# Reordering small VectorE, ScalarE and GpSimd work in a TensorE-bound decoder layer

## The chip, the cores and the metric

The kernel runs on one core of one Trainium2 chip. The metric is the device time of one execution in microseconds, as the median of three runs. A profile of one more execution gives the rows shown below.

## The reference

One decoder layer over x (512 tokens, 1024 features) and a memory of 256 rows, all in float32. Norms are RMS norms with a gain vector.

```
u = rms_norm(x, ln_mix_pre);  proj = u @ w_in            # q, k, v of three branches, three gates
y_swa = windowed attention (8 query heads, 2 key heads, sinks, relative bias)
y_sb  = stick-breaking attention (8 heads of 64):
        a = exp(log_sigmoid(z) + reverse cumulative sum of log_sigmoid(-z)), below the diagonal
y_mem = cross attention to rms_norm(mem, ln_mem) @ w_mem_kv (4 heads of 128)
merged = sum over the branches of sigmoid(gate_b) * (y_b @ w_branch_b)
h = x + rms_norm(merged @ w_out, ln_mix_post)
u = rms_norm(h, ln_ffn_pre)
a = silu(u @ w_gate) * (u @ w_up)
out = h + rms_norm(a @ w_down, ln_ffn_post)
```

## The kernel before

Every large product is taken as three products of float32r parts: each operand is split into a hi part (a copy by ScalarE, line 136) and a lo part (operand minus hi, by VectorE, line 137), and TensorE adds hi*hi, lo*hi and hi*lo into one PSUM bank (`mm3`, lines 168 to 170). Weights come from HBM as `raw` tiles of 512 KB, are split by `split` into `hi` and `lo`, and feed a `Stream` of units. A stream loads four units ahead, splits three ahead, and its generators yield the estimated time of each piece; `run(us)` takes pieces worth that many us, and `later(us, fn)` calls `fn` when the stream's own clock has gone on by `us`.

The order in which Python writes the instructions is a rank. A list scheduler with a cost model then gives each engine's order: whenever an engine is free in the plan, it takes the instruction of the highest rank that is ready in the plan. `after(a, b)` adds the order that `a` follows `b` without a wait of its own on the chip where both are on one engine. Only the start (`manual_schedule`, lines 725 to 776) keeps the written order.

The stages, in order:

- The start: ten warm-up products, then the first key projections `kb` chunk by chunk. `gained` scales a chunk of x by its gain on ScalarE to the hi part `uh` (line 246), and VectorE makes the lo part `ul` (line 247). `first_split` splits the first weights.
- Projections and eight stick-breaking heads. `sb_head` writes scores `z`, then for three tiles Abs, Exp and Ln on ScalarE, and on VectorE the term `e` (line 872), its hi part `sh` (line 877) and lo part `sl` (line 878). Then it yields 7.0 us, in which the stream's products are taken, and then multiplies `sh` and `sl` with triangular ones. In that stretch `st["chain"]` puts the weights' hi parts behind the head's last Ln. The projection's result is taken from its bank by line 299.
- Gates of the other two branches, by a scheme of seven products from quarter weights in 14 groups of 24 products per branch. Most quarter weights are sums, made by accumulating loads that GpSimd issues (`q_issue`, line 456). During the last branch's gates the loop over `outs` loads and splits `w_out` (`out_load` line 1056, `out_split`), two tiles at a step; then come the loads of x for the residual (`x_load`) and `bcast`, which loads a norm vector into all partitions by SP (line 1046, two tiles of 128x512) and scales it by -0.5 on GpSimd (line 1047).
- Branch products and `merge`. `branch_t` multiplies by the gate on VectorE (line 593) and adds the branches, mostly on GpSimd (line 596). `merge(h)` transposes, adds (line 611) and splits into `mgh` and `mgl` four times for each half `h`.
- The output product `mx` (`mix_mm`), two norms (`mix`), transposes, then gate and up products (`gx`, `gy`, `gw`) with 11 tile groups, again by seven products. `behind(act, dve)` puts later splits behind the two instructions given.
- The down product, seven products of six units each (`dn_mm`; banks `x`, `y`, `w`). Its left operand is split into `lh` and `ll` by `left_of`, three units ahead; its weights `bp` and `r` into hi and lo. `dn_end` combines the banks, and `dn_half` squares a half (line 1389), multiplies by the gain (line 1391 or 1395), and after the second half normalises and stores.

SP issues most loads in order; GpSimd issues the accumulating ones in the order of its own queue. The tag `ck` has 73 tiles of 128x512, shared by nearly everything.

Of the kernel before, what the change touches and what calls it, by code (L numbers as in the profile page):

```python
# [10 lines left out]
F32 = mybir.dt.float32  # L11
# [94 lines left out]
def tile_kernel(ctx, tc, a):  # L106
# [13 lines left out]
    def ck(name, dt=F32):  # L120
        return ckp.tile([P, 512], dt, tag="ck", name=name)
# [12 lines left out]
    def split(raw, hi, lo):  # L134

        ins = nc.scalar.copy(hi, raw)  # L136
        lows = nc.vector.tensor_tensor(lo, raw, hi.bitcast(F32), op=ALU.subtract)  # L137
        if "behind" in st:
            after(ins, st["behind"][0])
            after(lows, st["behind"][1])  # L140
        return ins
# [460 lines left out]
    def merge(h):  # L602

        for c in range(4):
            pt = (dps if (h, c) in ((1, 0), (1, 1)) else aps)(f"mg{h}{c}")
            for t in range(NT):
                nc.tensor.transpose(
                    pt[:, t * P : (t + 1) * P], gate_t[(MEM, t, h)][:, c * P : (c + 1) * P], ident[:, :]
                )
            acc = st[("acc", 4 * h + c)]  # L610
            nc.vector.tensor_tensor(acc[:, :], pt[:, :], acc[:, :], op=ALU.add)
            mh, ml = ck(f"mgh{h}{c}", F32R), ck(f"mgl{h}{c}", F32R)
            split(acc[:, :], mh[:, :], ml[:, :])
            merged[4 * h + c] = (mh, ml)

    for c in range(8):
        dn.add(a["w_p"][:, c].rearrange("p k n -> p (k n)"), 1024, proj("kb" if c < 4 else "qb", c % 4))
# [85 lines left out]

    def gain_split(k):
        h, l = ck(f"uh{k}", F32R), ck(f"ul{k}", F32R)
        gained(xraw[k][:, :], g_pre[:, k : k + 1], h[:, :], l[:, :])
        u[k] = (h[:, :], l[:, :])


# [15 lines left out]
    with tc.manual_schedule():  # L725

        idle = cst.tile([P, 512], BF16, name="idle")
        nc.vector.memset(idle[:, :], 0.0)
        pw = dps("warm")
        for i in range(WARM):  # L730
            mm(pw[:, :], idle[:, :P], idle[:, :], True, True)

        first_load(nc.scalar, 0)
        first_table = nc.scalar.preload_act_table_set("natural_log_exp_and_others")
        load_x(0, 3)
        first_load(nc.sync, 1)
        load_x(3, 5)
        first_load(nc.sync, 2)
        load_x(5, 8)
        dn.loaded = dn.have = FIRST  # L740
        for i in range(FIRST):
            first_split(i, 0)
            gain_split(i)
        for p in (1, 2):
            for i in range(FIRST):
                first_split(i, p)
            for k in range(*PIECE[p]):
                if u[k] is None:
                    gain_split(k)
        xacc = ck("xacc")  # L750
        nc.scalar.activation(xacc[:, :], xraw[0][:, :], AF.Square)
        for k in range(1, KC):
            nc.scalar.activation(xraw[k][:, :], xraw[k][:, :], AF.Square)
            nc.vector.tensor_tensor(xacc[:, :], xacc[:, :], xraw[k][:, :], op=ALU.add)
        dn.ahead(4, 3)

        for i in range(FIRST):
            first_ps[("kb", i)] = aps(f"kb{i}")
        order = [(0, 0, "hh"), (0, 0, "lh"), (1, 0, "hh"), (0, 0, "hl"), (1, 0, "hl"), (1, 0, "lh")]
        order += [(i, k, x) for i, k in ((0, 1), (1, 1), (2, 0), (2, 1)) for x in ("hh", "lh", "hl")]  # L760
        for i, k, x in order:
            w = (his if x[0] == "h" else los)[i]
            mm(first_ps[("kb", i)][:, :], w[:, k * P : (k + 1) * P], u[k][x[1] == "l"], k == 0 and x == "hh", False)
        gens = [dn.units[i]["mm"](his[i], los[i]) for i in range(FIRST)]
        for k in range(2, KC + 1):
            for g in gens:
                next(g, None)
        dn.at = FIRST
        st["rs"], st["rb"] = rstd_of("x", xacc, S, aps)
        st["chain"] = since[-1]  # L770
        for f in st.pop("waiting"):
            f()
# [65 lines left out]
    def sb_head(h):  # L838
        c = h // 2
        ks, qs, ql = (st[(x, c, h % 2)] for x in ("kbs", "qbs", "qbl"))  # L840
        z = [aps(f"z{h}{i}") for i in range(3)]

        def seg(ts, j):
            i, o, n = SEG[j]
            return ts[i][:, o : o + n]

        for j in range(4):
            i, o, n = SEG[j]
            kj = slice(j * P, (j + 1) * P)
            if j < 3:  # L850
                out, qh, qlo = z[i][:, o : o + n], qs[:, j * P :], ql[:, j * P :]
            else:

                out = z[i][:, o : o + 2 * n]
                qh = qs[:, j * P :].unsqueeze(1).to_broadcast([P, 2, P])
                qlo = ql[:, j * P :].unsqueeze(1).to_broadcast([P, 2, P])
            mm(out, ks[:, kj], qh, j < 3, False)
            mm(out, ks[:, kj], qlo, False, False)

        for i in range(2):  # L860
            mm(z[i][:, :P], identb[:, :], negm[:, :], False, False)
        blocks23 = z[2][:, :].rearrange("p (b n) -> p b n", b=4)[:, 0:4:2, :]
        mm(blocks23, identb[:, :], negm[:, :].unsqueeze(1).to_broadcast([P, 2, P]), False, False)
        e = [ck(f"e{h}{i}") for i in range(3)]
        sh = [ck(f"sh{h}{i}", F32R) for i in range(3)]
        sl = [ck(f"sl{h}{i}", F32R) for i in range(3)]
        for i in range(3):
            x, n = e[i][:, : W[i]], W[i]
            nc.scalar.activation(x, z[i][:, :n], AF.Abs)
            fn(x, x, AF.Exp, scale=-1.0)  # L870
            st["chain"] = fn(x, x, AF.Ln, bias=1.0)
            nc.vector.scalar_tensor_tensor(x, z[i][:, :n], 0.0, x, op0=ALU.max, op1=ALU.add)  # L872
            if i == 2:

                nc.vector.tensor_tensor(e[i][:, 384:], e[i][:, 128:256], e[i][:, 256:384], op=ALU.add)
                x, n = e[i][:, :], 512
            nc.vector.tensor_copy(sh[i][:, :n], x)
            nc.vector.tensor_tensor(sl[i][:, :n], x, sh[i][:, :n].bitcast(F32), op=ALU.subtract)
        yield 7.0

        def both(t):

            return t[2][:, :].rearrange("p (b n) -> p b n", b=4)[:, 0:4:3, :]


        for j in range(3):
            for t in (sh, sl):
                mm(z[j][:, : W[j]], ntri_r[:, :], t[j][:, : W[j]], False, j == 2 and t is sl)
        for t in (sh, sl):
            mm(z[0][:, 128:], none_r[:, :], seg(t, 1), False, False)  # L890
        for t in (sh, sl):
            mm(z[0][:, 256:], none_r[:, :], both(t), False, t is sl)
            mm(z[1][:, 128:384], none_r[:, :], both(t), False, t is sl)
        mm(z[2][:, 128:256], none[:, :], seg(e, 3), False, True)
        for i in range(3):
            fn(e[i][:, : W[i]], z[i][:, : W[i]], AF.Exp)
        yield 3.0 if h % 2 == 0 else 4.0
        if h % 2 == 0:
            st["even"] = e
            return  # L900


        ys = aps(f"ysb{c}")
        for j in (3, 2, 1, 0):
            for i, x in ((1, e), (0, st["even"])):
                mm(ys[64 * i : 64 * i + 64, j * P :], vcols(j, 128 + (2 * c + i) * 64), seg(x, j), j == 3, j == 0)
        pair_out(SB, c, ys)
# [478 lines left out]
    def dn_half(t, first, c, h):  # L1386

        f, j = ck(f"fg{t}{h}"), 0 if first else 1
        nc.scalar.activation(ck(f"sqr{t}{h}")[:, :], c[:, :], AF.Square, accum_out=ssd[t][:, j : j + 1])
        if first:  # L1390
            nc.vector.tensor_tensor(f[:, :], c[:, :], gain_out[h][:, :], op=ALU.mult)
            out1[t] = f
            return
        r = rstd_small(f"d{t}", ssd[t])
        nc.vector.tensor_tensor(f[:, :], c[:, :], gain_out[h][:, :], op=ALU.mult)
        for hh, o in ((1, out1[t]), (0, f)):
            nc.vector.scalar_tensor_tensor(o[:, :], o[:, :], r, hres[t][hh][:, :], op0=ALU.mult, op1=ALU.add)
            nc.sync.dma_start(a["out"][t * P : (t + 1) * P, hh * 512 : (hh + 1) * 512], o[:, :])
# [52 lines left out]
    for i, (h, q) in enumerate(outs):  # L1451
        out_load(h, q)
        dn.run(2.6)
        out_split(h, q)
        dn.run(2.6)
    for t in range(NT):
        x_load(t)
    gpost = bcast("g_post")
    gfpre = bcast("g_fpre")
    dn.until(f"branch{MEM}")  # L1460
    first.close()
    fp = ctx.enter_context(tc.tile_pool(name="fp", bufs=9, reuse_waits="tile"))
# [55 lines left out]
    table("natural_log_exp_and_others")  # L1518
    tmp = {}
    mix_mm(0, 0, 4)  # L1520
    merge(1)
    mix_mm(1, 0, 4)
    mix_mm(0, 4, KC)
    tmp[0] = mix(0)
# [130 lines left out]
```

## Time and profile before

| | |
|---|---|
| time, median of 3 runs | 802.61 us (802.03 to 803.16) |
| the profiled execution | 803.96 us, span 801.9 us |
| TensorE busy | 791.9 us, 99% of the span |
| VectorE, ScalarE, GpSimd busy | 608.0, 474.8, 105.2 us |
| granted TensorE clock | 0.998 of full speed |
| DMA | 123.43 MB, 154 GB/s in the mean |

A matmul's record is longer than the step to the next one, since products are pipelined. So TensorE's pauses are read from start to start, and the idle time in a bracket is shorter than the pause. An instruction of VectorE, ScalarE or GpSimd likewise begins a little before the one ahead of it ends. In the rows PE is TensorE, DVE VectorE, ACT ScalarE, POOL GpSimd and SP SyncE; a "q" behind an engine is its queue of DMA issues.

### The profile page before, as it was taken

The numbers are of one execution on the slowest core, as the hardware profiler recorded it, in microseconds if no ns is written. First come the engines' busy times: TensorE is split into PE (matmuls) and PEld (weight loads), VectorE is DVE, ScalarE is ACT, GpSimd is POOL, SyncE is SP. The second block draws the span as 40 slices with busy tenths as digits, with TensorE's granted clock in tenths as the row PEclk, the third lists the DMA queues.
The fourth block names the chain that finished last, engine by engine and source line by source line (L and its number), as shares of the span: only waits on it lengthen the run. The fifth ranks groups of instructions, "written<-read, shape, count | busy, mean of one in ns | idle before, by whom it ended". The sixth has DMA issues, their size and how long they took to land.

```text
span 801.9 us, 12466 instructions
## 1 busy us (share of the span) xinstructions
PE 791.9 (99%) x4694; PEld 695.8 (87%) x4694; DVE 608.0 (76%) x957; ACT 474.8 (59%) x847; POOL 105.2 (13%) x131
## 2 busy tenths in 40 slices
PE   9999999999999999999999999999999999999996
PEld 6899888778788888888888899999999999888785
DVE  6895878656578876766876679867676777898797
ACT  7562766546776587557823466655544444666573
POOL 1203300000020120002062100100100000215200
PEclk9999999999999999999999999999999999999999
DMA  8444535221572478339869707987777762949802
GB/s 298 134 133 124 202 106 148 64 74 57 171 167 58 79 137 212 73 77 242 290 203 289 133 5 184 266 237 184 184 182 184 183 158 64 220 106 241 182 0 105
DMA packets 42876, 123.43 MB, mean 154 GB/s; under 512 B 5056, under 2 KB 6768, under 8 KB 42816
## 3 DMA queue, kind: packets, MB, share of 16 engines
q1 hardware_dynamic: 30912, 86.32, 33.6%
q0 software_dynamic: 11472, 35.93, 24.3%
q8 instruction: 36, 0.59, 0.3%
q10 hardware_dynamic: 432, 0.39, 0.1%
q14 instruction: 24, 0.20, 0.1%
HBM read 116.85 MB, written 3.67 MB: 150 GB/s over the span
## 4 chain that ended last, share of the span: by engine, by line
PE 88%; DVE 5%; DMA 3%; issue 2%; ACT 1%; POOL 1%; DVEq 0%; POOLq 0%; ACTq 0%
PE gx L168 5%; PE gx L170 5%; PE gx L169 5%; PE z L180 4%; DMA bp<-in_w_dn 3%; PE gy L170 3%; PE gy L168 3%; PE gy L169 3%; PE br L168 3%; PE br L169 3%; PE br L170 3%; PE mx L170 2%; PE mx L169 2%; PE mx L168 2%; PE g L168 2%
## 5 line engine op out<-in xcount | busy, mean ns | idle before, releaser
L136 ACT CAST hi<-gw 128x1024 fp32r<-128x1024 f32 x77 | 79.9, 1048 | 83.5 <-DVE gw L1231 39.9
L137 DVE TENSOR_TENSOR lo<-gw,hi 128x1024 fp32r<-128x1024 f32 x77 | 93.8, 1227 | 32.4 <-ACT hi L136 32.4
L137 DVE TENSOR_TENSOR lo<-raw,hi 128x1024 fp32r<-128x1024 f32 (+2 forms) x76 | 91.8, 1208 | 33.8 <-ACT hi L136 33.4
L136 ACT CAST hi<-raw 128x1024 fp32r<-128x1024 f32 (+2 forms) x76 | 78.4, 1037 | 44.7 <-PE pv L170 10.7
L1213 POOL DMA_DIRECT2D gw<-in_w_gu x27 | 23.3, 920 | 196.5 <-DMA gw<-in_w_gu 71.4
L136 ACT CAST hi<-r 128x1024 fp32r<-128x1024 f32 (+1 forms) x24 | 23.5, 981 | 19.8 <-PE y L170 5.3
L168 PE MATMUL x<-hi,lh 128*128 128x512 f32 x88 | 34.4, 390 | 0.3 <-ACT lh L136 0.3
L169 PE MATMUL x<-lo,lh 128*128 128x512 f32 x88 | 34.3, 389 | 0.0
L170 PE MATMUL x<-hi,ll 128*128 128x512 f32 x88 | 34.2, 390 | 0.0
L137 DVE TENSOR_TENSOR lo<-r,hi 128x1024 fp32r<-128x1024 f32 (+1 forms) x24 | 27.2, 1132 | 3.6 <-ACT hi L136 3.5
L137 DVE TENSOR_TENSOR lo<-bp,hi 128x512 fp32r<-128x512 f32 x33 | 22.7, 719 | 7.0 <-ACT hi L136 6.8
L456 POOL DMA_DIRECT2D raw<-in_w_g x16 | 13.9, 868 | 106.7 <-DVE lo L137 92.9
L193 ACT ACTIVATE e<-e 128x384 f32<-128x384 f32 (+1 forms) x48 | 26.9, 561 | 1.5
L136 ACT CAST hi<-bp 128x512 fp32r<-128x512 f32 x33 | 19.4, 620 | 14.1 <-DMA bp<-in_w_dn 5.0
L872 DVE SCALAR_TENSOR_TENSOR e<-z,e 128x384 f32<-128x384 f32 (+1 forms) x24 | 14.3, 597 | 15.7 <-ACT e L193 15.7
L168 PE MATMUL g<-uh,hi 128*128 128x512 f32 x64 | 25.4, 398 | 0.0
L170 PE MATMUL g<-uh,lo 128*128 128x512 f32 x64 | 25.3, 396 | 0.0
L168 PE MATMUL gx<-B11h,hi 128*128 128x256 f32 x88 | 25.1, 285 | 0.2 <-ACT B11h L1142 0.2
L168 PE MATMUL gx<-T4h,hi 128*128 128x256 f32 x88 | 25.1, 285 | 0.0
L169 PE MATMUL g<-ul,hi 128*128 128x512 f32 x64 | 25.0, 391 | 0.0
L170 PE MATMUL gy<-N22h,lo 128*128 128x256 f32 x88 | 25.0, 284 | 0.0
L168 PE MATMUL gy<-N22h,hi 128*128 128x256 f32 x88 | 25.0, 284 | 0.0
(792 smaller groups left out, 2831.5 us busy)
## 6 DMA issues: line engine op xcount, KB each, us to landing
gw<-in_w_gu SPq DMA_DIRECT2D x57, 512.0 KB, 4.9
gw<-in_w_gu POOLq DMA_DIRECT2D x27, 512.0 KB, 7.3
raw<-in_w_p SPq DMA_DIRECT2D x22, 512.0 KB, 3.7
raw<-in_w_g POOLq DMA_DIRECT2D x16, 512.0 KB, 6.1
raw<-in_w_g SPq DMA_DIRECT2D x12, 512.0 KB, 3.6
bp<-in_w_dn SPq DMA_DIRECT2D x22, 256.0 KB, 11.2
r<-in_w_dn POOLq DMA_DIRECT2D x10, 512.0 KB, 9.2
raw<-in_w_brt SPq DMA_DIRECT2D x8, 512.0 KB, 4.4
```

What stands on the lines that cost most here:

```text
L136: ins = nc.scalar.copy(hi, raw)
L137: lows = nc.vector.tensor_tensor(lo, raw, hi.bitcast(F32), op=ALU.subtract)
L168: one = nc.tensor.matmul(out, lh, rh, start=start, stop=False, skip_group_check=True)
L169: nc.tensor.matmul(out, lh, rl, start=False, stop=False, skip_group_check=True)
L170: return one, nc.tensor.matmul(out, ll, rh, start=False, stop=stop, skip_group_check=True)
L180: return nc.tensor.matmul(out, l, r, start=start, stop=stop, skip_group_check=True)
L193: ins = nc.scalar.activation(*args, **kw)
L456: nc.gpsimd.dma_start(t[:, :], src, accum_op=ALU.add)
L872: nc.vector.scalar_tensor_tensor(x, z[i][:, :n], 0.0, x, op0=ALU.max, op1=ALU.add)
L1213: nc.gpsimd.dma_start(gw[(n, key)][:, :], g_src(n, i, j), accum_op=ALU.add)
```

## The change

Five places change.

1. `split` puts the lo part behind `st["sums"]`, the last `sl` of a head, while that is set; `sb_head` sets it with each `sl` and takes it away after its 7.0 us.
2. `merge` splits by itself and gives back its last hi and lo instruction, and the second merge's go to `behind`, so that later splits follow them on ScalarE and VectorE.
3. The first chunk of x is scaled to its hi part by VectorE; VectorE then makes the first weights' lo part, and then the chunk's lo part.
4. In `dn_half` the square and the gain product of a half that comes first go into `rest`, which the stream calls 6.0 us of its clock later.
5. The norm vectors `g_post` and `g_fpre` are loaded and scaled after the second step of the loop over `outs` and no longer after `x_load`.

```
@@ split
         lows = nc.vector.tensor_tensor(lo, raw, hi.bitcast(F32), op=ALU.subtract)
+        if "sums" in st:
+            after(lows, st["sums"])
         if "behind" in st:
@@ merge
-            split(acc[:, :], mh[:, :], ml[:, :])
+            hi = nc.scalar.copy(mh[:, :], acc[:, :])
+            lo = nc.vector.tensor_tensor(ml[:, :], acc[:, :], mh[:, :].bitcast(F32), op=ALU.subtract)
             merged[4 * h + c] = (mh, ml)
+        return hi, lo
@@ gain_split
-        gained(xraw[k][:, :], g_pre[:, k : k + 1], h[:, :], l[:, :])
+        x, g = xraw[k][:, :], g_pre[:, k : k + 1]
+        if k == 0:
+
+            nc.vector.tensor_scalar(h[:, :], x, g, None, op0=ALU.mult)
+            first_split(0, 0)
+            nc.vector.scalar_tensor_tensor(l[:, :], x, g, h[:, :].bitcast(F32), op0=ALU.mult, op1=ALU.subtract)
+        else:
+            gained(x, g, h[:, :], l[:, :])
@@ the start
         for i in range(FIRST):
-            first_split(i, 0)
+            if i > 0:
+                first_split(i, 0)
             gain_split(i)
@@ sb_head
-            nc.vector.tensor_tensor(sl[i][:, :n], x, sh[i][:, :n].bitcast(F32), op=ALU.subtract)
+            st["sums"] = nc.vector.tensor_tensor(sl[i][:, :n], x, sh[i][:, :n].bitcast(F32), op=ALU.subtract)
         yield 7.0
+        st.pop("sums")
@@ dn_half
-        nc.scalar.activation(ck(f"sqr{t}{h}")[:, :], c[:, :], AF.Square, accum_out=ssd[t][:, j : j + 1])
+
+        def square():
+            nc.scalar.activation(ck(f"sqr{t}{h}")[:, :], c[:, :], AF.Square, accum_out=ssd[t][:, j : j + 1])
+
         if first:
-            nc.vector.tensor_tensor(f[:, :], c[:, :], gain_out[h][:, :], op=ALU.mult)
+
+            def rest():
+                square()
+                nc.vector.tensor_tensor(f[:, :], c[:, :], gain_out[h][:, :], op=ALU.mult)
+
+
+            fs.later(6.0, rest)
             out1[t] = f
             return
+        square()
         r = rstd_small(f"d{t}", ssd[t])
@@ the loop over outs
         out_split(h, q)
         dn.run(2.6)
+        if i == 1:
+            gpost = bcast("g_post")
+            gfpre = bcast("g_fpre")
     for t in range(NT):
         x_load(t)
-    gpost = bcast("g_post")
-    gfpre = bcast("g_fpre")
@@ after the branches
     mix_mm(0, 0, 4)
-    merge(1)
+    behind(*merge(1))
     mix_mm(1, 0, 4)
```

## Rows read from the trace of the kernel before

**Rows 1.** The page's first part: busy us, share, instructions.

```profile
PE 791.9 (99%) x4694; PEld 695.8 (87%) x4694; DVE 608.0 (76%) x957; ACT 474.8 (59%) x847; POOL 105.2 (13%) x131
```

**Rows 2.** Timeline of TensorE, sixth stick-breaking head: start, us, line, out<-in.

```profile
167.72 0.40 PE L180 MATMUL z<-sh,none_r 128*128 128x256 f32 x2
169.18 0.44 PE L180 MATMUL z<-sl,ntri_r 128*128 128x384 f32 x1 [1.06 <-DVE sl L878]
```

**Rows 3.** Timeline of VectorE in the same head.

```profile
167.31 1.22 DVE L137 TENSOR_TENSOR lo<-raw,hi 128x1024 fp32r<-128x1024 f32 x1
168.44 0.68 DVE L878 TENSOR_TENSOR sl<-e,sh 128x512 fp32r<-128x512 f32 x1
```

**Rows 4.** Timeline of TensorE after the first merge.

```profile
419.46 0.39 PE L169 MATMUL mx<-wo03l,mgh 128*128 128x512 f32 x1
420.19 0.50 PE L170 MATMUL mx<-wo03h,mgl 128*128 128x512 f32 x1 [0.34 <-DVE mgl L137]
```

**Rows 5.** Timeline of VectorE after the first merge.

```profile
417.58 1.09 DVE L137 TENSOR_TENSOR mgl<-g,mgh 128x512 fp32r<-128x512 f32 x1
418.60 0.68 DVE L593 TENSOR_TENSOR gq2p<-br,gq2p 128x512 f32<-128x512 f32 x1
419.20 0.93 DVE L137 TENSOR_TENSOR mgl<-g,mgh 128x512 fp32r<-128x512 f32 x1
```

**Rows 6.** Timeline of GpSimd after the first merge.

```profile
415.45 1.66 POOL L596 TENSOR_TENSOR gq2p<-gq2p,gq0p 128x512 f32<-128x512 f32 x1 [1.75 <-DVE gq2p L593]
417.08 1.93 POOL L1047 TENSOR_SCALAR bc_g_post<-bc_g_post 128x512 f32<-128x512 f32 x1
418.98 3.10 POOL L1047 TENSOR_SCALAR bc_g_fpre<-bc_g_fpre 128x512 f32<-128x512 f32 x2
```

**Rows 7.** Timeline of ScalarE in the down product, from the first squares.

```profile
755.44 0.63 ACT L1389 ACTIVATE sqr<-p 128x512 f32<-128x512 f32 x1
...
756.67 0.60 ACT L136 CAST hi<-bp 128x512 fp32r<-128x512 f32 x1
757.18 0.61 ACT L136 CAST lh<-aq 128x512 fp32r<-128x512 f32 x1
```

**Rows 8.** Timeline of TensorE in the down product, the same stretch.

```profile
757.18 0.39 PE L170 MATMUL x<-hi,ll 128*128 128x512 f32 x1
757.85 0.50 PE L168 MATMUL x<-hi,lh 128*128 128x512 f32 x1 [0.28 <-ACT lh L136]
...
758.91 0.40 PE L168 MATMUL x<-hi,lh 128*128 128x512 f32 x1
```

**Rows 9.** The chain that ended last, its first 7 us: start, us, what.

```profile
1.35 4.45 PE warm L180 x10
5.80 1.28 PE kb L180 x3
```

**Rows 10.** Timeline of ScalarE at the start.

```profile
4.50 0.72 ACT L246 ACTIVATE uh<-xg 128x512 fp32r<-128x512 f32 x1
```

**Rows 11.** Timeline of ScalarE behind the second merge.

```profile
435.45 0.60 ACT L1100 ACTIVATE mt<-mx 128x512 f32<-128x512 f32 x1 [5.88 <-PE mx L170]
```

**Rows 12.** Windows: stretch, busy us by engine, clock, DMA share, GB/s.

```profile
375.00:380.00 5.00, 5.00 (x23) 4.14 (x23) 3.60 (x5) 2.77 (x4) 0.81 (x1) 1.00 1.07 212
```

**Rows 13.** Timeline of GpSimd in the last gates: first and last of six.

```profile
360.91 0.86 POOL L456 DMA_DIRECT2D raw<-in_w_g  x1 [15.88 <-DVE lo L137]
...
374.95 0.86 POOL L456 DMA_DIRECT2D raw<-in_w_g  x1 [2.29 <-DVE lo L137]
```

**Rows 14.** Timeline of ScalarE in the last gates.

```profile
383.23 1.06 ACT L136 CAST hi<-raw 128x1024 fp32r<-128x1024 f32 x1
```

**Rows 15.** Instructions on the gates' banks: count, ns min/median/max, first to last start.

```profile
L168 PE MATMUL g2p<-hi,uh x32: 389/389/500, 355.3 to 393.0; 128*128 128x512 f32 x32
```

**Rows 16.** Line 1046, the norm vectors' loads, from issue to landing.

```profile
DMA to landing us min/median/max: 3.7/4.8/9.8
```

**Rows 17.** Timeline of SP's queue in the last gates.

```profile
358.26 2.88 SPq L1056 DMA_DIRECT2D wo<-in_w_out  x6
```

## The prediction

> **What bounds the kernel now.** I read the page's engine shares first, then TensorE product by product, then the other engines in the places where TensorE stood still. TensorE is busy for 791.9 of 801.9 us, and no other engine comes near [rows 1]. So whatever does not shorten a pause of TensorE is worth nothing, and an edit can cost only by making a pause. Products of 512 columns start 0.23 us after one another, those of 256 columns 0.12 us; a larger step is a pause. Behind the start, three places have pauses over 0.4 us that this change touches, and they are the terms of the sum. The profiled execution took 803.96 us, its span 801.9, so 2.1 us lie around it; it is 1.35 us above the median of the runs, 802.61, and I take the sum off both alike.
>
> **Lo parts behind a head's last sum.** In the sixth stick-breaking head TensorE starts a 256-column product pair at 167.72, could go on at 167.96, and starts the next product at 169.18, released by VectorE's last sum `sl` [rows 2]. VectorE did a weight's lo part first, at 167.31, and `sl` at 168.44 [rows 3]. The edit makes lo follow `sl`: `sl` starts 1.13 us sooner, so TensorE would go on at 168.05. The gain is 1.13, between 1.06 (the wait in the bracket) and 1.22 (the whole pause). The lo sits in the same place in all eight heads, but in the other seven TensorE had other products meanwhile, so nothing comes of it there. The price is a lo 0.7 us later. Behind it wait the reuse of its raw buffer by SP's next load and its own products, three units (72 products of 0.23 us) on, so that lateness is covered; uncovered, it would be 0.7 us per head. The plan also sees each `sl` earlier and may put its product earlier in TensorE's order; order and arrival then move by the same lo, and I count nothing.
>
> **Norm vectors scaled sooner.** `mx<-wo03h,mgl` starts 0.73 us after the product before it, 0.50 more than the step, and waits for VectorE's fourth `mgl` of the first merge [rows 4]. That `mgl` took 0.93 and the third 1.09, while `L593` between them took 0.68 [rows 5]; an undisturbed 128x512 subtract such as `sl` takes 0.68 [rows 3]. GpSimd scaled the norm vectors during both slow ones, from 417.08 and from 418.98 [rows 6]. Without them the two save 0.41 + 0.25 = 0.66 us, more than the 0.50 that are missing: gain 0.50. Both ends: nothing, if something else takes GpSimd's time there (its add at 415.45 stays), and 0.66. The Trainium skill (SBUF — State Buffer, section "SBUF: two separate sides") says that VectorE instructions with two SBUF inputs and GpSimd's take one shared port in turn and hold it for a whole instruction; the slow subtracts have two SBUF inputs, `L593` reads a PSUM bank and was not slowed, so the rows agree. By that rule a `mgl` could be blocked for a whole scaling, 1.93 us, and the sum would be larger than by the rows' 0.66; the rows decide.
>
> In the new place, in the stage before, four loads of 256 KB and four scalings of about 1.5 us (two took 3.10 [rows 6]) come among the accumulating loads of the gates' weights. I cost them at nothing, with this cover: the DMA engines are full there (share 1.07 at 212 GB/s [rows 12]), so 1.05 MB puts later transfers back by 4.9 us. Six accumulating loads are issued by GpSimd from 360.91 to 374.95 [rows 13]. The hi part of the last starts at 383.23 [rows 14], so it had landed; with its 1.06 and a lo of 1.22 it is done at 385.5. TensorE takes 14 groups of 24 products from 355.3 on, 2.72 each [rows 15], so it reaches the last group at 390.7. The cover is 5.2 us; the others are spaced alike. 4.9 fits, barely. What goes over 5.2 is a pause, one for one.
>
> **Conversions held behind the second merge.** The first hi and lo parts of the feed-forward weights move behind the second merge's eight parts. No pause follows the second merge now; ScalarE then idles 5.88 us before the first square [rows 11], which takes the two moved hi parts (1.05 each). VectorE's moved lo parts fit the same idle time. Cost and gain 0; without the idle time 2.1 us on the first norm's chain.
>
> **Squares held back.** The product at 757.85 starts 0.67 after its predecessor, and the next three take 1.06 instead of 0.68 [rows 8]: 0.44 + 0.38 = 0.82 us lost, since `lh` began only at 757.18. Two squares and their reads took ScalarE from 755.44 to 756.67, ahead of a hi and of that `lh` [rows 7]. Put behind them, they let `lh` start 1.23 us sooner, at 755.95 and end at 756.56, and TensorE wanted it at 757.41. Gain 0.82; both ends 0 (if the squares stay ahead) and 0.82. Their own time falls later, where ScalarE converts ahead of need; their result is wanted only when the last two products of the down projection end. The second pair moves likewise; no pause stands there.
>
> **First chunk on VectorE.** TensorE runs its ten warm-up products until 5.80 and goes straight into `kb` [rows 9]; ScalarE's scaled chunk was there at 5.22 [rows 10]. VectorE takes between nothing and 0.68 (the two-operand `sl` of the same shape [rows 3]) and still ends before 5.80. Gain 0: the warm-up hides it. If VectorE's lo of the chunk came later by the whole 0.68, the same products would still be ahead of it in TensorE's order.
>
> **Sum.** 1.13 + 0.50 + 0.82 = 2.45: span 799.4, profiled execution 801.5, median 802.61 - 2.45 = 800.2.
>
> **The rivals.** *One gain is lost, or its pause comes back next door.* The list scheduler that orders each engine by a plan orders anew after every edit. Held-back squares are only lower in rank: if ScalarE has nothing else ready in the plan, they stay ahead of `lh` and that part of the change does not do what it says (801.0). A lo shifted in another head, or a product planned too early, makes a pause of up to 1.2 us, the largest that a misplaced lo makes now (801.4). For it: the plan has put the lo ahead of `sl` in all eight heads, so it misjudges. Against it: the same misjudgement cost TensorE time in one of eight. I say 801.2.
>
> *The broadcasts crowd the gates' weights.* GpSimd's scalings wait for their loads, and accumulating loads behind them on GpSimd's queue wait too. SP issues six `wo` loads from 358.26 within 2.88 us [rows 17]; behind the first four of these the broadcasts would be out by 361.9. Earlier they landed after 4.8 us in the median and 9.8 at most [rows 16]. With 4.8 the scalings are done at 372.9, with 9.8 at 377.9. The six issues are some 2.8 us apart: ahead of the sixth (374.95) nothing comes of it, ahead of the fourth (369.3) lateness is 3.6 or 8.6, ahead of the third (366.5) 6.4 or 11.4; less 5.2 that is a pause of 0, 3.4, 1.2 or 6.2 us. Middle of this case: 2.2 us, 802.4. *Slower* comes out only when the pause is over 2.45 + 1.6 = 4.05 us, so from the third issue on and with the slow landing: 800.2 + 6.2 = 806.4. For it: the full DMA engines. Against it: the scalings are written after the code that issues these loads, and GpSimd has gaps of some 2 us between the issues. The Trainium skill (DMA: Bandwidth & Descriptors, section "Issuing engines are not separate DMA queues") says that transfers of SP and GpSimd share the same 16 engines and interleave; by it the broadcasts do slow the accumulating loads even on another queue, as this rival has it, and the share of 1.07 with both at work agrees.
>
> **How the numbers follow.** All three gains: 0.52, 800.2, its own range 799.3 to 801.0. One lost or come back: 0.22, 801.2. Broadcasts cost part: 0.13, 802.4. Broadcasts cost over 4 us: 0.09, 806.4. Something quicker than the sum: 0.04. 0.2% is 1.6 us, about what a measurement here can tell: faster is under 801.0, slower over 804.2. Faster takes the first, the last and a small part of the second case: 0.58. Same: the rest of the second and most of the third, 0.29. Slower: the fourth and the upper tail of the third, 0.13. The range goes from 799.3, the sum with its upper ends (1.22 + 0.66 + 0.82 = 2.70) and 0.6 for the scatter of the runs, to 802.9, which takes in the second case and the middle of the third.
>
> **What would show it.** In the changed profile: the last `sl` of each head straight behind its `sh`, and no wait of TensorE for `sl` in the sixth head; the `mgl` subtracts at 0.68 but for the one under GpSimd's add, and no wait for `mgl`; `lh` ahead of the squares and no wait for it near 757; `kb` still at 5.8. It is wrong if products of the gate stage pause between 360 and 395, if a new wait for `sl` or for a weight's hi or lo part stands in another head, or if the squares stand where they stood.

## The result, and the profile after

The kernel became slower: 806.0 us in the median of 6 runs (805.71 to 807.97) against 802.9 us for the kernel before in 6 runs beside it, ratio 1.0043 [1.003, 1.0056]. The forecast was 800.2. TensorE stays the bound; it is busy a little longer, and the others hardly change (the page's first part, kernel after; compare [rows 1]).

```profile
PE 792.4 (99%) x4694; PEld 696.2 (87%) x4694; DVE 609.7 (76%) x958; ACT 473.8 (59%) x846; POOL 105.3 (13%) x131
```

So the time again lies in TensorE's pauses. Its waits in the kernel after (what waited, for whom: total us, times, longest):

```profile
PE g2p L170 <- ACT gq2p L546: 2.4, 2, 1.8
...
PE ysb L182 <- ACT e L195: 1.1, 1, 1.1
```

Neither stood among the waits of before. Those for `sl` [rows 2], `mgl` [rows 4] and `lh` [rows 8] are gone. To see what each place is worth I took, for every product, the step from its start to the next start less the usual step of its kind (the median in before of products of the same shape), and added up by stretch (after minus before):

| stretch, us | after minus before, us | what stands there |
|---|---|---|
| 0 to 10 | -0.87 | TensorE's slow products at the start (last section) |
| 130 to 150 | +1.53 | fourth head, wait for `e` |
| 160 to 170 | -1.00 | sixth head, `sl` |
| 240 to 250 | -0.41 | a pause near 246 that edit 1 takes along |
| 370 to 400 | +4.68 | gates: wait for `gq2p`, and slow products behind it |
| 410 to 430 | -0.65 | first merge, `mgl` |
| 750 to 760 | -0.85 | down product, `lh` |

Two of the gains are partly the luck of the one profiled execution of before: the first and the last differ from run to run, as shown below. These rows come to +2.4 and the rest of the span to -0.2; the spans differ by 2.3 (804.2 against 801.9). Without the first row it is +3.1, and with the last one at the 0.4 that the medians below give for it, +3.6; the medians differ by 3.1.

**The gates.** Timeline of TensorE after (start, us, line, out<-in, idle before <-releaser):

```profile
370.56 0.39 PE L172 MATMUL g2p<-hi,xsp51l 128*128 128x512 f32 x1
372.73 0.50 PE L170 MATMUL g2p<-hi,xsp30h 128*128 128x512 f32 x1 [1.78 <-ACT gq2p L546]
...
373.53 0.63 PE L170 MATMUL g2p<-hi,xsp30h 128*128 128x512 f32 x1
373.95 0.63 PE L171 MATMUL g2p<-lo,xsp30h 128*128 128x512 f32 x1
...
376.94 0.40 PE L172 MATMUL g2p<-hi,xsp30l 128*128 128x512 f32 x1
```

The step from 370.56 to 372.73 is 2.17, so 1.94 us are lost. Then, from 373.53 to 376.94, eight products start 0.43 apart in place of 0.23: another 1.6 us. The windows of the same stretch show it in the column of the granted clock (behind the five engines, ahead of the DMA share): 0.95 and 0.71, where before has 1.00 in both.

```profile
369.00:374.00 5.00, 3.22 (x14) 2.34 (x13) 1.23 (x1) 2.02 (x3) 0.31 (x2) 0.95 1.07 246
374.00:379.00 5.00, 5.00 (x17) 3.97 (x16) 3.56 (x4) 3.13 (x4) 2.64 (x3) 0.71 1.09 238
```

A step of 0.43 is TensorE's lower level, 1.2 GHz, against 0.23 at 2.4; the pause of 1.94 us came before the fall.

The wait is for a copy of a finished bank to SBUF by ScalarE (`gq2p<-g2p`), which the next product group needs before it may write that bank again. Timeline of ScalarE after, then of ScalarE and of TensorE before:

```profile
371.15 1.04 ACT L136 CAST hi<-raw 128x1024 fp32r<-128x1024 f32 x1 [3.78 <-DMA raw<-in_w_g]
372.10 1.07 ACT L546 COPY gq2p<-g2p 128x512 f32<-128x512 f32 x2
```

```profile
369.20 1.05 ACT L136 CAST hi<-raw 128x1024 fp32r<-128x1024 f32 x1 [0.95 <-PE g2p L170]
370.50 0.59 ACT L544 COPY gq2p<-g2p 128x512 f32<-128x512 f32 x1 [0.25 <-PE g2p L170]
371.86 0.59 ACT L544 COPY gq2p<-g2p 128x512 f32<-128x512 f32 x1 [0.77 <-PE g2p L170]
```

```profile
371.67 0.39 PE L168 MATMUL g2p<-hi,xsp30h 128*128 128x512 f32 x1
```

In both, the hi part of a gate weight stands ahead of the two copies on ScalarE. Before, it starts at 369.20 and the copies follow their banks at once. After, ScalarE stands idle 3.78 us for that weight's load, and the copies behind it run only from 372.10, though the first one's bank had its last product at 369.20. The weight's own products come much later (in before at 377.11); it is what stands behind its hi part that was urgent.

The sizes fit. In before the hi part ends at 370.25, the first copy takes from 370.50 to 371.09, and TensorE writes that bank again at 371.67: the hi part can be 0.25 + 0.58 = 0.83 us late before TensorE pauses. Measured against the product that waits, it starts 2.83 us later in after, and 1.69 and 2.75 us later in two kernels below (the norm vectors alone, their loads alone). Less 0.83 that is 2.00, 0.86 and 1.92 us; the pauses there are 1.94, 0.81 and 1.87. The stage pauses a second time at 390.87, by 0.74 us, for a copy that ran at 391.20 behind three conversions.

The load is late because of the moved ones. SP issues them here (timeline of SP after):

```profile
359.28 0.90 SPq L1059 DMA_DIRECT2D bc_g_post<-in_g_post  x2
360.28 1.04 SPq L1059 DMA_DIRECT2D bc_g_fpre<-in_g_fpre  x2
```

DMA issues from 355 to 385 (queue, count, KB, median us from issue to landing), after and then before:

```profile
raw<-in_w_g POOLq DMA_DIRECT2D x6, 512.0 KB, 10.9
```

```profile
raw<-in_w_g POOLq DMA_DIRECT2D x6, 512.0 KB, 7.2
```

The accumulating loads land 3.7 us later, in DMA engines that were full already [rows 12]; the first of the six, for which the hi part above waits, lands after 11.0 us against 8.2. The first four were not issued late (timeline of GpSimd after, against [rows 13]), the last two some 2 us, and the scalings come behind all six:

```profile
360.04 0.86 POOL L458 DMA_DIRECT2D raw<-in_w_g  x1 [15.88 <-DVE lo L137]
...
368.20 0.86 POOL L458 DMA_DIRECT2D raw<-in_w_g  x1 [1.02 <-DVE lo L137]
...
377.54 3.32 POOL L1060 TENSOR_SCALAR bc_g_post<-bc_g_post 128x512 f32<-128x512 f32 x2
```

**The sixth head** went as forecast: `sl` comes straight behind `sh` and TensorE's step of 1.46 [rows 2] is 0.44 (timelines of VectorE and of TensorE after):

```profile
167.58 0.43 DVE L889 CAST sh<-e 128x512 fp32r<-128x512 f32 x1
168.05 0.69 DVE L890 TENSOR_TENSOR sl<-e,sh 128x512 fp32r<-128x512 f32 x1
```

```profile
168.35 0.39 PE L182 MATMUL z<-sh,none_r 128*128 128x256 f32 x2
168.79 0.45 PE L182 MATMUL z<-sl,ntri_r 128*128 128x384 f32 x1
```

**The fourth head** has a new pause, a step 1.28 us over the usual one, as the product into `ysb` waits for the last `e` of ScalarE (TensorE after; before, a projection product `qa` stood there and the sum over `ysb` came later):

```profile
135.47 0.38 PE L182 MATMUL z<-e,none 128*128 128x128 f32 x2
136.97 0.66 PE L182 MATMUL ysb<-e,v_all 128*64 128x128 f32 x6 [1.12 <-ACT e L195]
```

```profile
136.35 0.38 PE L180 MATMUL z<-e,none 128*128 128x128 f32 x2
136.49 0.48 PE L168 MATMUL qa<-uh,hi 128*128 128x512 f32 x1
```

**First merge and down product** (VectorE, then ScalarE, after). The `mgl` subtracts take 0.68 each, not 1.09 and 0.93 [rows 5]. The two squares, one behind the other ahead of `hi` and `lh` in [rows 7], are parted: one follows a `hi`, the second comes behind two more and an `lh`:

```profile
417.56 1.28 DVE L616 TENSOR_TENSOR mgl<-g,mgh 128x512 fp32r<-128x512 f32 x2
...
419.36 0.68 DVE L616 TENSOR_TENSOR mgl<-g,mgh 128x512 fp32r<-128x512 f32 x1
```

```profile
757.60 0.62 ACT L136 CAST hi<-bp 128x512 fp32r<-128x512 f32 x1 [1.34 <-DMA bp<-in_w_dn]
758.13 0.63 ACT L1404 ACTIVATE sqr<-p 128x512 f32<-128x512 f32 x1
...
760.77 0.40 ACT L136 CAST lh<-aq 128x256 fp32r<-128x256 f32 x1
761.08 0.63 ACT L1404 ACTIVATE sqr<-p 128x512 f32<-128x512 f32 x1
```

TensorE's products step 0.23 through this stretch.

### The profile page after: what moved, and what is told of

It reads as the page before. It is cut to its first block, busy times and chain, and to the rows that moved or that the text cites. A ratio compares the mean times of both kernels' runs of the same rounds, so it can differ in the third digit from the quotient of the medians.

```text
span 804.2 us, 12466 instructions
## 1 busy us (share of the span) xinstructions
PE 792.4 (99%) x4694; PEld 696.2 (87%) x4694; DVE 609.7 (76%) x958; ACT 473.8 (59%) x846; POOL 105.3 (13%) x131
## 4 chain that ended last, share of the span: by engine, by line
PE 93%; DMA 2%; DVE 2%; ACT 1%; issue 1%; DVEq 0%; SPq 0%; ACTq 0%
PE gx L170 5%; PE gx L172 5%; PE gx L171 5%; PE z L182 3%; PE br L170 3%; PE br L171 3%; PE br L172 3%; PE gy L172 3%; PE gy L170 3%; PE gy L171 3%; PE x L171 2%; PE x L172 2%; PE x L170 2%; PE mx L172 2%; PE mx L171 2%; PE mx L170 2%
## 5 line engine op out<-in xcount | busy, mean ns | idle before, releaser
L172 PE MATMUL gw<-B21h,lo 128*128 128x256 f32 x88 | 25.0, 284 | 0.0
```

Source lines behind the costliest of these rows:

```text
L172: return one, nc.tensor.matmul(out, ll, rh, start=False, stop=stop, skip_group_check=True)
```

## The experiments

The theory: the norm vectors' loads alone cost about 4 us, by way of the copies behind a waiting hi part, and the other four edits together gain little, because the sixth head's gain is given back in the fourth. The rivals: the scalings on GpSimd cost it and not the loads; the loss is spread over other edits too; the pause in the gates stays whatever stands there.

**Norm vectors alone, and all but the norm vectors.** The first is before with this hunk alone, the second is after without it.

```
@@ the loop over outs
+        if i == 1:
+            gpost = bcast("g_post")
+            gfpre = bcast("g_fpre")
     for t in range(NT):
         x_load(t)
-    gpost = bcast("g_post")
-    gfpre = bcast("g_fpre")
```

> The kernel before with the norm vectors' loads and scalings moved, and nothing else. Theory A: the loads lie among the accumulating loads of the last gates, one of these lands over 2 us later, the hi part that waits for it holds ScalarE's queue, and a copy of a finished bank stands behind it; TensorE then pauses between 365 and 395 for about 4.5 us with the half clock that follows, and the pause for mgl (0.65 us) goes: 806.8 us. Rival B: the pauses in the gates come from a new order that the other edits bring; then only the mgl pause goes here: 802.3 us.

> The changed kernel with the norm vectors' loads and scalings back where they were. Theory A: no pause between 365 and 395, the pause for mgl is back, 806.0 - 4.6 + 0.65 = 802.0 us. Rival B (the new order of the other edits makes the pauses in the gates): they stay, near 806 us.

Measured: 806.26 us, 1.0044 [1.0031, 1.0056], for the norm vectors alone; 802.47, 0.9995 [0.9986, 1.0004], for the rest. The one hunk carries the whole loss. Its longest wait:

```profile
PE g2p L168 <- ACT gq2p L544: 3.1, 3, 1.8
```

The total came as expected, but not by the expected way: the gates pause three times, by 0.81, 2.00 and 0.80 us, each time for a copy, and no half clock follows the longest one (TensorE, then the windows, with the granted clock at 1.00):

```profile
382.73 0.39 PE L170 MATMUL g2p<-hi,xsp61l 128*128 128x512 f32 x1
384.95 0.50 PE L168 MATMUL g2p<-hi,uh 128*128 128x512 f32 x1 [1.84 <-ACT gq2p L544]
```

```profile
385.00:390.00 5.00, 5.00 (x22) 4.16 (x23) 3.99 (x7) 3.97 (x7) 0.00 (x0) 1.00 0.94 342
```

In the rest the gates have 0.2 us of that wait, with the accumulating loads landing after 7.5 us in the median; the `mgl` wait is back, and the fourth head's pause is still there:

```profile
PE ysb L182 <- ACT e L195: 1.1, 1, 1.1
PE mx L172 <- DVE mgl L616: 0.3, 1, 0.3
PE g2p L170 <- ACT gq2p L546: 0.2, 1, 0.2
```

**The sums' order alone, the first chunk alone, the squares alone.** Before with the hunks of `split` and `sb_head`; with those of `gain_split` and the start; with that of `dn_half`.

> The kernel before with lo parts behind a head's last sum, and nothing else. Theory A: the sixth head's pause of 1.2 us shrinks to 0.2, and the fourth head gets the new pause of 1.3 us before ysb that the changed kernel has, since the plan takes the products of sl earlier and leaves none to fill in: 802.9 - 1.0 + 1.4 = 803.3 us. Rival: the fourth head's pause comes from another edit; then 801.9 us.

> The kernel before with the first chunk of x scaled by VectorE, and nothing else. Theory A: the warm-up hides it, the first key projections come earlier only where the granted clock happens to rise earlier in an execution: 802.9 us as before. Rival: the 0.87 us that the changed kernel's profile gained by the end of the first projections belong to this edit: 802.0 us.

> The kernel before with the held-back squares, and nothing else. Theory A (the pause near 757 was long in the first profile because a load of bp came late in that one execution; other profiles of the same order show 0.1 to 0.7 us): gain 0.1 to 0.5, 802.6 us. Rival B (the whole 0.82 us, each time): 802.1 us.

Measured: 803.18, 1.0007 [0.9998, 1.0016]; 803.29, 1.0003 [0.9994, 1.0012]; 802.45, 0.9995 [0.9986, 1.0004]. None can be told from no change. With the sums' order the sixth head's wait is gone and the fourth head's `ysb` wait is there. With the first chunk nothing moves in the gates or heads. With the squares the `lh` wait is gone.

**Loads moved, scalings left.** `bcast` without its scaling at the new place, and the four scalings where they stood, behind `x_load`:

```
+        if i == 1:
+            gpost = bcast("g_post", False)
+            gfpre = bcast("g_fpre", False)
     for t in range(NT):
         x_load(t)
-    gpost = bcast("g_post")
-    gfpre = bcast("g_fpre")
+    halve(gpost, nc.gpsimd)
+    halve(gfpre, nc.gpsimd)
```

> The kernel before with the norm vectors' four loads moved, while GpSimd's scalings stay where they were. Theory A (the loads alone crowd the accumulating ones): the gates pause as with both moved, and the mgl pause of 0.65 us is back: 806.3 + 0.6 = 806.9 us. Rival B (GpSimd's scalings in the gates hold up its queue or VectorE): no pause in the gates, 802.9 us.

Measured: 806.81, 1.0043 [1.0031, 1.0056], the whole loss again, with 3.9 us of waits for the copies. The rank of the scalings did not hold them: they ran right behind the last accumulating load, as they do with both moved (GpSimd's timeline), so the `mgl` pause is gone here too. The 806.9 of the expectation was therefore met partly by luck: it counted that pause as back.

```profile
378.05 3.32 POOL L1056 TENSOR_SCALAR bc_g_post<-bc_g_post 128x512 f32<-128x512 f32 x2
```

GpSimd issued the accumulating loads at 360.66, 364.12, 366.93, 368.82, 374.29 and 377.48, ahead of any scaling. The rival that makes the scalings the cause by way of GpSimd's queue is out: no load stood behind one, and the pause at 371.19 came before the first scaling.

**The hi part behind the copies.** After, with the first p6 weight split two units ahead and not three, which puts its hi part behind the copies at 370:

```
             ):
                 dn.units[g0 + g][what].append(lambda f=f, args=args: f(*args))
+        if b == MEM:
+            dn.units[g0 + 5]["split_ahead"] = 2
```

> The changed kernel, but in the last gates the hi part of the first p6 weight is written behind the copies of the finished p5 banks, so that ScalarE copies first. Theory A (the late load pauses TensorE only through the copy that stands behind the waiting hi part on ScalarE): the 1.9 us pause at 370 and the half clock behind it (together 3.7 us) go, a smaller pause may come back where the weight itself is then late: 802.3 to 803.5 us. Rival B (TensorE lacks the weight itself): the pause stays and comes some us later, 806 us.

Measured: 807.24, 1.0046 [1.0034, 1.0058]. The time missed the expectation, and by the number alone it is on rival B's side; the timelines show why (ScalarE, then TensorE):

```profile
370.50 0.59 ACT L546 COPY gq2p<-g2p 128x512 f32<-128x512 f32 x1 [2.25 <-PE g2p L172]
372.34 1.05 ACT L136 CAST hi<-raw 128x1024 fp32r<-128x1024 f32 x1
...
383.81 1.04 ACT L136 CAST hi<-raw 128x1024 fp32r<-128x1024 f32 x1 [1.40 <-DMA raw<-in_w_g]
384.76 0.61 ACT L136 CAST wo02h<-wo 128x512 fp32r<-128x512 f32 x1
385.28 0.61 ACT L136 CAST wo03h<-wo 128x512 fp32r<-128x512 f32 x1
385.80 0.57 ACT L546 COPY gq2p<-g2p 128x512 f32<-128x512 f32 x1
```

```profile
382.31 0.39 PE L172 MATMUL g2p<-hi,xsp61l 128*128 128x512 f32 x1
386.43 0.79 PE L170 MATMUL g2p<-hi,uh 128*128 128x512 f32 x1 [3.73 <-ACT gq2p L546]
```

The copy at 370.50 is on time and the pause there is gone, as the mechanism says. But the loads are as late as ever, and at the next bank the same thing stands in the same order: a copy behind a hi part that waited for its load, and behind two `w_out` conversions. TensorE waits 3.73 us, and the granted clock from 387 to 392 is 0.73. The place moved, the cause did not. What rival B gives as the reason is not seen: the product at 386.43 waits for a copy and not for its weight. No run puts every copy of the stage ahead of the hi parts, so what the late loads would cost in that order is not shown.

**The loads sooner, where the DMA engines have room.** `bcast` between the two pairs of memory heads, edit 5 alone otherwise:

```
     for h in (0, 2):
         for us in mem_pair(h):
             dn.run(us)
+        if h == 0:
+            gpost = bcast("g_post")
+            gfpre = bcast("g_fpre")
...
-    gpost = bcast("g_post")
-    gfpre = bcast("g_fpre")
```

> The kernel before with the norm vectors' loads and scalings moved still earlier, between the two pairs of memory heads, where SP issues them near 325 us and the DMA engines are a third busy. Theory A (only the full DMA engines make the move dear): no pause in the last gates, the 0.65 us pause for mgl gone: 802.9 - 0.65 = 802.2 us. Rival B (four tiles held early, or the scalings on GpSimd, cost the same wherever they stand): pauses in the gates of 3 us and more, 805.5 us or more.

Measured: 802.78, 0.9996 [0.9987, 1.0005]. SP issues them at 333.82, in a stretch with a DMA share of 0.49, and the accumulating loads of 355 to 385 land after 7.7 us in the median, against 7.2 and 10.9 above (windows and DMA issues):

```profile
330.00:340.00 10.00, 10.00 (x59) 8.78 (x58) 8.21 (x13) 5.06 (x13) 3.04 (x3) 1.00 0.49 111
```

```profile
raw<-in_w_g POOLq DMA_DIRECT2D x6, 512.0 KB, 7.7
```

The 4 us are gone, and so is the wait for `mgl`; a wait of 0.4 us for a copy near 387 is one that the sums' order alone has as well, without any load moved. The same bytes and scalings, held even longer, cost nothing where the loads find room, so rival B is out. Its profiled execution has a wait of 0.6 for `lh`, which hides the `mgl` gain in its span; the gain of 0.5 is below what the median tells.

**Which head brings the fourth head's pause.** Edit 1 in all heads but the fourth, and in the sixth alone; `last` is the `sl` instruction:

```
+        if h != 3:            (the other kernel: if h == 5:)
+            st["sums"] = last
         yield 7.0
+        st.pop("sums", None)
```

> The kernel before with lo parts behind the last sum in every head but the fourth. Theory A (the fourth head's new pause comes from its own reordering): the sixth head keeps its 1.0 us, the fourth head has no pause: 802.9 - 1.1 - 0.4 (the pause near 246 that went with the edit alone) = 801.4 us. Rival B (the plan shifts everything and makes a pause in some other head): 802.9 us or more.

> The kernel before with the lo parts behind the last sum in the sixth head alone. Theory A (the fourth head's pause comes from the plan of the heads ahead of it, which this leaves as it was): the sixth head's pause shrinks by 1.0 us and no pause comes in the fourth: 801.9 us. Rival B (what is gained there is given back in a later head): 802.9 us.

Measured: 802.85, 0.9996 [0.9987, 1.0004], and 801.63, 0.9986 [0.9978, 0.9995]. Without edit 1 in the fourth head, its pause stays; with edit 1 in the sixth alone, it is gone (timelines of TensorE, in this order):

```profile
136.34 0.38 PE L182 MATMUL z<-e,none 128*128 128x128 f32 x2
137.84 0.44 PE L182 MATMUL ysb<-e,v_all 128*64 128x128 f32 x4 [1.12 <-ACT e L195]
```

```profile
135.78 0.38 PE L182 MATMUL z<-e,none 128*128 128x128 f32 x2
135.92 0.48 PE L170 MATMUL qa<-uh,hi 128*128 128x512 f32 x1
```

My theory that the fourth head's own reordering puts `ysb` too early fell. The pause needs the edit in some of the other heads, the sixth apart, which shifts the plan. That these are heads ahead of the fourth is likely from the order of time; no run here shows it, or which of them.

**What can be kept.** Edits 2, 3 and 4, the norm loads at their old place but scaled by ScalarE behind the second merge, and edit 1 in all heads but the fourth; then the same with edit 1 in the sixth alone:

```
-    merge(1)
+    behind(*merge(1))
+    halve(gpost, nc.scalar)
+    halve(gfpre, nc.scalar)
```

> The kernel before with: lo parts behind the last sum but in the fourth head, first chunk on VectorE, held-back squares, later splits behind the second merge, and the norm vectors loaded where they were but scaled by ScalarE behind the second merge. Theory A: the pauses in the sixth head (1.0), for mgl (0.65), near 246 (0.4) and for the squares (0.1 to 0.8) go and none comes: 800.5 us. Rival B: the new order brings a pause of the size that it takes, 802.5 us.

> As the run named best, but the lo parts stand behind the last sum in the sixth head alone. Theory A: the fourth head's 1.4 us pause goes too: 802.05 - 1.4 = 800.7 us. Rival B: another order brings a pause back: 802 us.

Measured: 802.05, 0.9988 [0.998, 0.9997], and 801.26, 0.9979 [0.9971, 0.9988]. The first missed its 800.5 and is nearer to the rival's 802.5, since it still has the `ysb` wait; in the second, behind the start, TensorE's longest wait for an engine is 0.2 us, for a copy `gq2p`.

The second beats both kernels, and it is 4.7 us under the changed one.

## Why the prediction was wrong, point by point

**The step that failed** is the cover of the moved loads: "The cover is 5.2 us; the others are spaced alike. 4.9 fits, barely." The delay was sized fairly: 4.9 us, of which 3.7 arrived in the median at the accumulating loads and 2.8 at the first. The cover was measured to the wrong consumer. I took the time until TensorE wants the weight; the hi part's real neighbour is the next instruction on ScalarE's queue, a copy that frees a PSUM bank. Before, the hi part starts at 369.20 and takes 1.05, the copy behind it is due at 370.50, and TensorE wants the copied bank at 371.67: 0.83 us of slack, not 5.2. The rows that tell it are ScalarE's from 369 to 372 in before; the prediction rested on the one at 383.23 [rows 14]. It also counted "a pause, one for one"; here 1.94 us of pause were followed by 1.6 us that products at half pace cost, though not so with the norm vectors alone. The prediction named what is queued behind a waiting instruction for GpSimd's queue, and not for ScalarE's. Its groups of 24 products, and those of the text ahead of it, are of 12: TensorE does 168 products in the 14 groups. The 2.72 us per group came from the start times, so the 5.2 stand as they were meant.

**The rival** "The broadcasts crowd the gates' weights" (0.13 and 0.09) had the stage and the sign. Its path was wrong: it let the scalings hold GpSimd's queue, and they held nothing. That its 806.4 is close to the 806.0 measured is luck. The sentence on shared DMA engines that stood beside it did the work: by the Trainium skill (DMA: Bandwidth & Descriptors, section "Issuing engines are not separate DMA queues") SP's and GpSimd's transfers interleave on the same engines, and the landing times, 7.2 us without and 10.9 with the broadcasts, agree.

**Edit 1.** The term of 1.13 was right for the sixth head (1.00 came off its stretch, and 1.2 us off the median when it was made there alone: 802.83 to 801.63). In all heads it is nothing, 803.18: the rival "its pause comes back next door", with a price of up to 1.2, is what happened, at 1.28 in the fourth head. I gave it 0.22 and argued that the plan's misjudgement cost one head of eight; the edit touched the plan of all eight for the sake of one.

**Norm vectors and `mgl`.** Gain 0.50 forecast; the stretch from 410 to 430 lost 0.65 less. That step was right.

**Squares.** One square of the two still stands early, the other is held back as forecast, and the pause is gone in every kernel with edit 4. The term of 0.82 was mis-sized: kernels without the edit have lost 1.15, 0.70, 0.34, 0.14, 0.08 or nothing there, by execution; before's profile, with 0.82, was at the upper end. Alone it gave 0.4 in the medians, inside the interval.

**Conversions behind the merge, and the first chunk.** Both 0, as forecast, as far as the runs can tell: the first chunk alone is 1.0003, and the merge's order, not run alone, shows no wait in the stretch behind it.

So the sum as it should have stood, in us of the median: gates +4.68, the two heads and the pause near 246 +0.12, `mgl` -0.65, squares -0.4, the rest of the span -0.2: +3.6. The medians give 3.1, and the interval of the ratio reaches from 2.4 to 4.5.

## What to carry to other kernels

When transfers are put among others, ask first which conversion will wait for the late one, and then what stands behind that conversion on its engine: the slack is that of the most urgent instruction in the queue, not that of the data that is late. Look for a stretch where the DMA share has room before moving bytes (0.49 here cost nothing, 1.07 cost 4 us). And where a list scheduler orders anew, make an edit in the one place that needs it: the same line in one head gained 1.2 us, in eight heads nothing.

## What the runs showed of the hardware that was not expected

In the changed kernel a pause of 1.94 us in a stream of otherwise dense products was followed by a fall of the granted clock to 1.2 GHz: it printed 0.71 over the next 5 us, and eight products stepped 0.43. The length of the pause alone does not tell when this happens. With the norm vectors alone a pause of 2.00 us was followed by a granted clock of 1.00 and steps of 0.23, and so were pauses of 1.87 and 1.77 us with their loads alone; the one of 3.89 us, with the hi part behind the copies, was followed by 0.73. What decides it, no run here shows.

At the start, TensorE's full pace comes at a different time in each execution, whatever the edit. All begin the ten warm-up products at 1.35. The sixth `kb` product starts at 7.57 in before and at 6.66 in after, 0.91 us apart; but the four kernels with edit 3 and not edit 5 have 6.79, 7.45, 7.03 and 6.80, the run with the hi part behind the copies, which starts as after does, has 7.58, and norm vectors alone, the loads between the memory heads and the sixth head alone, all without edit 3, have 7.00, 6.87 and 6.61. In before the products step 0.43 ahead of that point and 0.23 behind it, which is how the two levels show; the column of the granted clock prints 1.00 there in before and in after. The Trainium skill (TensorE: Matmul & The Clock Gate, section on the HAM clock gate) says that the number of slow products at a start varies from run to run; these rows agree. So a single profile of this kernel can differ by 0.9 us for this alone, which is why the first row of the table above is no gain of edit 3.

GpSimd's scalings slow VectorE in the new place too: the subtract `wo11l` (128x512, at 377.19) took 1.85 us and a lo (128x1024, at 378.97) 2.10, against 0.68 and 1.22 for the same shapes undisturbed [rows 3]; TensorE waited for neither.
